# Expert weight loads of one expert with 8 KiB runs, in place of loads of two experts with 4 KiB runs

## The chip, the core and the metric

The program runs on one core of a Trainium2 chip. A core has the matrix engine (TensorE, PE in the profile, with its weight loads as PEld), the vector engine (DVE), the scalar engine (ACT), GpSimd (POOL) and the sync engine (SP), which here issues the DMAs; 16 DMA engines move the data. The metric is the device time of one execution in microseconds, 1385.64 us as the median of three.

## What is computed

Two layers of a decoder trunk on 512 tokens of 1024 channels. Each layer is a mixer (layer 0: gated mixing and a short convolution, layer 1: a gated linear recurrence) followed by a mixture of experts: 32 experts in 4 groups, each token goes to the two best experts of its best group. All weights are float32. The part that the change touches is the experts:

```python
def expert_block(args):                       # 128 slots of tokens, their gates, one expert
    tok_b, g_b, e = args
    xb = x_pad[tok_b]
    hid = jax.nn.silu(xb @ w_gate[e]) * (xb @ w_up[e])
    return (hid @ w_down[e]) * g_b[:, None].astype(xb.dtype)
# w_gate, w_up: (2, 32, 1024, 512); w_down: (2, 32, 512, 1024); the sum over a token's two slots is added to x
```

An expert's weights are three matrices of 2 MiB each. Both layers together read 2 x 32 x 6 MiB = 384 MiB of them; the mixers' weights are some 27 MiB.

## The kernel before

**Pairs.** Every expert has 64 slots for tokens, and two experts share one tile of 128 slots: `NPAIR` = 16 pairs a layer, numbered here from 0 to 15. `experts` (line 1057) works one pair: eight rows of `gate` into bank `pg`, eight of `up` into `pu`, the product `hid` (line 1072, one DVE instruction a pair), four transposes to `hT`, and four rows of `down` into `pd`, each row in two column halves. A row is what one partition holds of one contraction step: channel `8 p + j` for gate and up (`(p j)` with 8 rows of 512 numbers, 2 KiB each), `4 p + j` for down (4 rows of 1024 numbers, 4 KiB). `two` (line 1052) does both experts for one row: the expert `s` gets the partitions `64 s` to `64 s + 63` of the output, so every row needs the weights of both experts. Each call is one instruction in the program and two in the profile. Between `up` and `down` PE does work without weights: `gather` collects the tokens of the next pairs (`px`), `combine` adds the results of the pair before to the tokens (`pc`).

**Loads.** `moe_stream` (line 70) lists the loads of a layer in the order of use, `prefetch` (line 107) issues them on SP as buffers come free, `take` (line 126) hands the next one to the work and `done` (line 138) returns buffers and issues again. A load is 1 MiB: of both experts of a pair, two rows of gate or up, or one row of down. In DRAM these are two runs of 4 KiB a partition. A pair takes 12 loads: 4 gate, 4 up, 4 down. They lie in a ring of 12 buffers (10 of the tag `w`, and `D0`, `D1`; the first loads of a layer also use `Q` and `X`), and each buffer is returned when PE has done the load's rows. SP's queue is in order: it waits at the first load that has no buffer. In pair 0 gate and up are mixed by the table `FIRST`, since its tokens are gathered meanwhile. In the last pair `stop_at` keeps the next layer's loads back. `overflow` (line 1187) is a loop for experts with more than 64 tokens; it uses loads of its own, and the packets of the trace leave no room for a pass of it (126896 on the issue queue, all told for by the loads and stores outside of it).

The instructions stand in the order in which the program is written; there is no scheduler behind it.

Of the kernel before, what the change touches and what calls it, by code (L numbers as in the profile page):

```python
# [22 lines left out]
NJ = 8  # L23
NE = 32
CAP = 64
NPAIR = NE // 2
# [13 lines left out]
def hybrid_trunk(ctx: ExitStack, tc: tile.TileContext, x, norm_mix_g, norm_ffn_g, norm_final_g,  # L40
# [13 lines left out]
    def bank(i, name, shape=(P, 512), dtype=F32):  # L54
        return ps.tile(list(shape), dtype, tag=f"b{i}", name=name)
# [7 lines left out]
    def units(kind, u, src, slot="w"):  # L63
# [3 lines left out]
        for i in range(n):  # L67
            stream.append((kind, u, src[:, i * k:(i + 1) * k, :], slot))

    def moe_stream(l):  # L70
        slots = ["D1"] + ["w"] * RING + ["Q", "X"] + (["D0", "D1"] + ["w"] * RING) * (NPAIR + 1)
        n = 0
        for i in range(NPAIR):
            parts = [(w, NJ, t) for w in (moe_w_gate, moe_w_up) for t in range(4)]
            if i == 0:
                parts = [parts[k] for k in FIRST]
            for w, k, t in parts + [(moe_w_down, 4, t) for t in range(4)]:
                rows_of_both = w[l, 2 * i:2 * i + 2].rearrange("e (p j) f -> p e j f", j=k)
                stream.append(("moe", i, rows_of_both[:, :, t * k // 4:(t + 1) * k // 4, :], slots[n]))
                n += 1  # L80

    Y0 = (4, 5, 6, 7, 0, 1, 2, 3)
    Y1 = tuple(range(NJ))
# [54 lines left out]
    def done(n=1):  # L138

        for _ in range(n):  # L140
            free[used.popleft()] += 1
        prefetch()
# [614 lines left out]
    class Moe:  # L757
# [291 lines left out]
                G.tensor_tensor(self.rows[:, c, :].rearrange("t (p j) -> t j p", j=NJ), f(self.xh)[:, c],  # L1049
                                f(self.xl)[:, c], op=OP.add)  # L1050

        def two(self, o, xt, w, j, first, last, wide):
            for s in range(2):
                TE.matmul(o[64 * s:64 * s + 64, :], xt[:, 64 * s:64 * s + 64], w[s][:, j, wide],  # L1054
                          start=first, stop=last)

        def experts(self, xt, by, weights, done, between, during=lambda k, j: None, n=2, mixed=False, out="Q"):

            pg, pu = bank(0, "pg"), bank(1, "pu")
            for k, j in [divmod(n * part + i, NJ) for part in (FIRST if mixed else range(2 * NJ // n)) for i in range(n)]:  # L1060
                if j % n == 0:
                    w = weights(k, j // n)
                during(k, j)
                self.two((pg, pu)[k], xt()[:, j], w, j % n, j == 0, j == NJ - 1, slice(0, 512))
                if j % n == n - 1:
                    done()
                if (k, j) == (0, NJ - 1):
                    between(0)
                    sg = big.tile([P, 512], F32, tag="w1", name="sg")
                    A.activation(sg, pg, AF.Silu, scale=by(1))  # L1070
            hid = big.tile([P, 512], F32, tag="w2", name="hid")
            V.scalar_tensor_tensor(hid, pu, by(1), sg, op0=OP.mult, op1=OP.mult)  # L1072
            between(1)
            ptr = bank(4, "pth", (P, 4, P))
            for k in range(4):
                TE.transpose(ptr[:, k, :], hid.rearrange("s (f k) -> s k f", k=4)[:, k, :], ident)
            hT = big.tile([P, 4, P], F32, tag="w3", name="hT")
            A.copy(hT, ptr)  # L1078
            between(2)
            pd = [bank(2 + s, f"pd{s}") for s in range(2)]  # L1080
            for k in range(4):
                for s in range(2):
                    if n == 1:
                        w = weights(2, 2 * k + s)
                    elif s == 0:
                        w = weights(2, k)
                    self.two(pd[s], hT[:, k], w, 0, k == 0, k == 3,
                             slice(512 * s, 512 * s + 512) if n > 1 else slice(0, 512))
                done()
            between(3)  # L1090
            y = four(T, "y", F32R, out)
            yh, yl = y[0:2], y[2:4]
            for s in range(2):
                A.activation(yh[s], pd[s], AF.Copy, scale=by(0))  # L1094
                V.scalar_tensor_tensor(yl[s], pd[s], by(0), f(yh[s]), op0=OP.mult, op1=OP.subtract)  # L1095
            return yh, yl

        def blocks(self, after):

            steps = []  # L1100
            n_over = None
            for p in range(NPAIR):
                q, r = divmod(p, 2)
                sp = []
                if p == NPAIR - 1:

                    stop_at[0] = min(stop_at[0], pos[1] + 12 + AHEAD)

                rows = [lambda j=j: self.gather(q + 1, j)
                        for j in (range(4 * r, 4 * r + 4) if p > 1 else range(NJ) if p else ())] if q < NQ - 1 else []

                def whole(n):

                    for _ in range(n):
                        if rows:
                            rows.pop(0)()
                        if steps:
                            steps.pop(0)()  # L1120

                def during(k, j):
                    if (p, k, j) == (0, 1, 3):
                        self.gate_values()
                    if p == 0 and k == 0 and j % 2 == 0:
                        for i in (j, j + 1):
                            self.gather(0, i)

                def between(n):
                    if n == 0:  # L1130
                        if p == 0:
                            self.by_slot()
                        if r == 0 and q < NQ - 1:
                            self.spread(q + 1)
                        return
                    if n == 3 and self.l == 0 and p in (3, 4, 5):
                        lambda_constants(p - 3)
                    if n == 1:
                        for _ in range(min(2, len(rows))):
                            rows.pop(0)()  # L1140
                        if steps:
                            steps.pop(0)()
                    if n == 2:
                        while rows or steps:
                            whole(1)
                    if n == 3 and p == NPAIR - 1:
                        self.before_overflow()
                    if n == 3:
                        sp.append(self.place(pidx[:, p:p + 1], "w0" if p < NPAIR - 1 else "D0"))
                    if p == 0 and n == 1:  # L1150
                        self.slot_rows()
                        self.extras()

                if p == 3:
                    n_over = nc.values_load(self.cnt_i[0:1, 0:1], min_val=0, max_val=NOV // 2,
                                            skip_runtime_bounds_check_because="it is a sum of eight comparisons")
                def weights(k, part):
                    both = take("moe", p)
                    return [both[:, s] for s in range(2)]

                y = self.experts(lambda: self.xt[q][:, :, r * P:(r + 1) * P], lambda g: self.gs[:, g, p:p + 1],
                                 weights, done, between, during, mixed=p == 0)
                steps = self.combine(sp[0], *y, after if p == NPAIR - 1 else None)
                if p == NPAIR - 2 and self.l:
                    self.gain = gain_row(112, 6, "J")
            self.overflow(n_over)
            stop_at[0] = len(stream)
            free["D0"] = free["D1"] = free["Q"] = free["X"] = 0
            free["C1"] = 1
            prefetch()  # L1170
            warm(AF.Sqrt)
            for t in steps:
                t()
# [13 lines left out]
        def overflow(self, n_over):  # L1187

            slot, by, col, nxt, eid = self.walk
            with tc.For_i(0, n_over, 1):  # L1190
# [10 lines left out]
                for j in range(NJ):  # L1201
                    self.gather(NQ, j, P, lambda c: so[c // 2][:, c % 2])

                def loaded(k, part):
                    src, n = ((moe_w_gate, NJ), (moe_w_up, NJ), (moe_w_down, 4))[k]
                    j, h = (part, 0) if k < 2 else divmod(part, 2)
                    w = []
                    for s in range(2):
                        w.append(big.tile([P, 1, 512], F32, tag=f"sm{s + 1}", name="wo"))
                        e = src[self.l][bass.ds(ids[s], 1)].rearrange("o (p j) f -> p (o j) f", j=n)  # L1210
                        SY.dma_start(w[s], e[:, j:j + 1, 512 * h:512 * h + 512])
                    return w

                for t in self.combine(self.place(col), *self.experts(lambda: self.xt[NQ], lambda g: by[:, g, 0:1], loaded,
                                                         lambda: None, lambda n: None, n=1, out="C0")):
                    t()
                V.tensor_scalar(slot, slot, float(P), None, op0=OP.subtract)
                V.tensor_scalar(col, col, float(P), None, op0=OP.add)
# [175 lines left out]
```

## Time and profile before

| what | us |
|---|---|
| median of three runs | 1385.64 (1383.78 to 1388.72) |
| the profiled execution | 1385.47 |
| its span, first to last instruction | 1383.8 |
| PE busy | 1319.3 |
| DVE, ACT busy | 586.9, 347.2 |

The span is that of the profiled execution; 1.7 us lie around it. The expert stages take about 200 to 690 us (layer 0) and 890 to 1380 us (layer 1), the mixers the rest. In a window's row the letter x stands before the number of instructions, and matmuls are pipelined with their ends modelled, so a busy PE need not be a PE at its peak. A DMA share of 1.03 comes from packets that overlap on their engine.

### The profile page before, as it was taken

How to read it: one execution, taken by the hardware profiler on the slowest of the kernel's cores; microseconds unless marked ns; L12 is line 12 of the kernel's file. 1: busy time of each engine (PE TensorE's matmuls, PEld its weight loads, DVE VectorE, ACT ScalarE, POOL GpSimd, SP SyncE). 2: the span in 40 equal slices, each digit the busy share in tenths (PEclk: the TensorE clock that was granted, in tenths of full speed). 3: DMA queues.
4: the chain of work that ended last, by engine and by line, in shares of the span. 5: the costliest groups of instructions: out<-in, count | busy, mean ns of one | idle time of the engine just before them, and what ended most of it. 6: DMA issues, size and time to landing. Idle time of an engine off the chain costs nothing. (4 is left out here: it accounts for less than half of the span.)

```text
span 1383.8 us, 16540 instructions
## 1 busy us (share of the span) xinstructions
PE 1319.3 (95%) x6654; PEld 756.5 (55%) x6654; DVE 586.9 (42%) x1126; ACT 347.2 (25%) x581; POOL 49.4 (4%) x43
## 2 busy tenths in 40 slices
PE   9999999999999999998799999899999999999995
PEld 7888874554444544443486678545444454444432
DVE  6455462334323242322477873723333233323225
ACT  4335331121111211110246663212111111111113
POOL 0000200000000000000101001300000000000001
PEclk9999999999999999999899999999999999999998
DMA  9621169899999999999770035598999999999994
GB/s 358 202 97 61 61 230 339 346 410 408 410 409 409 409 409 409 409 409 409 274 267 0 0 143 202 207 347 335 409 410 408 409 409 409 409 409 409 409 409 161
DMA packets 126980, 436.95 MB, mean 316 GB/s; under 512 B 11316, under 2 KB 14000, under 8 KB 126896
## 3 DMA queue, kind: packets, MB, share of 16 engines
q1 hardware_dynamic: 126896, 435.82, 81.0%
q8 instruction: 55, 0.90, 0.3%
q14 instruction: 29, 0.24, 0.0%
HBM read 433.69 MB, written 2.10 MB: 315 GB/s over the span
## 5 line engine op out<-in xcount | busy, mean ns | idle before, releaser
L1054 PE MATMUL pu<-w,xt 128*64 128x512 f32 x1024 | 234.0, 597 | 20.7 <-DMA w<-in_moe_w_up_dram 19.3
L1054 PE MATMUL pg<-w,xt 128*64 128x512 f32 x1024 | 228.8, 597 | 3.7 <-ACT xt L916 2.5
L1054 PE MATMUL pd<-w,hT 128*64 128x512 f32 x1024 | 226.8, 595 | 1.4 <-ACT hT L1078 1.4
L1072 DVE SCALAR_TENSOR_TENSOR hid<-pu,gs,sg 128x512 f32<-128x512 f32 x32 | 24.0, 751 | 365.3 <-PE pu L1054 246.2
L1054 PEld LDWEIGHTS pu<-w,xt 128*64 128x64 f32 x1024 | 69.8, 137 | 178.1 <-issue 118.5
L1054 PEld LDWEIGHTS pg<-w,xt 128*64 128x64 f32 x1024 | 72.6, 137 | 147.5 <-issue 133.9
L1054 PEld LDWEIGHTS pd<-w,hT 128*64 128x64 f32 x1024 | 70.7, 137 | 140.4 <-issue 129.4
L916 ACT ACTIVATE xt<-px,gcol 128x256 f32<-128x256 f32 x128 | 60.7, 475 | 301.5 <-PE px L914 301.5
L913 PE MATMUL px<-st,xh 128*128 128x256 f32 x512 | 132.4, 294 | 1.9 <-DVE st L903 1.5
L914 PE MATMUL px<-st,xl 128*128 128x256 f32 x512 | 126.3, 282 | 0.0
L913 PEld LDWEIGHTS px<-st,xh 128*128 128x128 f32 x512 | 97.4, 190 | 30.9 <-issue 27.0
L1094 ACT ACTIVATE y<-pd,gs 128x512 fp32r<-128x512 f32 x64 | 43.8, 687 | 264.6 <-PE pd L1054 263.2
L1095 DVE SCALAR_TENSOR_TENSOR y<-pd,gs,y 128x512 fp32r<-128x512 f32 x64 | 47.8, 750 | 140.5 <-ACT y L1094 138.0
L1039 DVE TENSOR_TENSOR xT<-pc,xT 128x512 f32<-128x512 f32 x128 | 81.4, 684 | 57.1 <-PE pc L1038 57.1
L1039 DVE TENSOR_TENSOR rows<-pc,rows 128x512 f32<-128x512 f32 x128 | 81.1, 684 | 53.2 <-PE pc L1038 53.2
L914 PEld LDWEIGHTS px<-st,xl 128*128 128x128 f32 x512 | 97.5, 190 | 1.6
L405 DVE TENSOR_TENSOR wl<-w,wh 128x512 fp32r<-128x512 f32 x89 | 60.9, 687 | 51.9 <-PE pu L450 26.8
L1038 PE MATMUL pc<-sp,y 128*128 128x512 f32 x256 | 69.8, 406 | 4.7 <-issue 4.7
L404 ACT CAST wh<-w 128x512 fp32r<-128x512 f32 x94 | 58.0, 620 | 63.9 <-PE pu L450 37.7
L1070 ACT ACTIVATE sg<-pg,gs 128x512 f32<-128x512 f32 x32 | 22.0, 688 | 193.3 <-PE pg L1054 186.2
L1038 PE MATMUL pc<-y,sp 128*128 128x512 f32 x256 | 67.4, 395 | 2.0 <-DVEq L1190 2.0
L737 PE MATMUL po<-y,wh 128*128 128x512 f32 (+1 forms) x288 | 67.6, 376 | 0.7 <-ACT y L479 0.7
(264 smaller groups left out, 1357.4 us busy)
## 6 DMA issues: line engine op xcount, KB each, us to landing
w<-in_moe_w_gate_dram SPq DMA_DIRECT2D x128, 1024.0 KB, 18.3
w<-in_moe_w_up_dram SPq DMA_DIRECT2D x128, 1024.0 KB, 18.4
w<-in_moe_w_down_dram SPq DMA_DIRECT2D x128, 1024.0 KB, 18.3
w<-in_ab_w_in_dram SPq DMA_DIRECT2D x10, 1024.0 KB, 15.7
w<-in_c_w_in_dram SPq DMA_DIRECT2D x8, 1024.0 KB, 10.8
w<-in_ab_w_out_dram SPq DMA_DIRECT2D x4, 1024.0 KB, 10.0
w<-in_c_w_out_dram SPq DMA_DIRECT2D x4, 1024.0 KB
xin<-in_x_dram SPq DMA_DIRECT2D x4, 512.0 KB, 6.4
```

Of the source, the lines that this page charges most:

```text
L404: A.copy(wh, w)
L405: lo.tensor_tensor(wl, w, f(wh), op=OP.subtract)
L737: TE.matmul(o[m, i], w[:, kk, :], part(js[4 * kh + kk])[:, h], start=kh + k + kk == 0, stop=(kh, k, kk) == (1, 2, 3))
L913: TE.matmul(px, self.xh[:, c, j, :], st(c), start=(c == 0), stop=False)
L914: TE.matmul(px, self.xl[:, c, j, :], st(c), start=False, stop=(c == NT - 1))
L916: A.activation(self.xt[q][:, j, :], px, AF.Copy, scale=g)
L1038: TE.matmul(pc, a, b, start=(n == 0), stop=(n == 1))
L1039: V.tensor_tensor(d, pc, d, op=OP.add)
L1054: TE.matmul(o[64 * s:64 * s + 64, :], xt[:, 64 * s:64 * s + 64], w[s][:, j, wide], start=first, stop=last)
L1072: V.scalar_tensor_tensor(hid, pu, by(1), sg, op0=OP.mult, op1=OP.mult)
L1094: A.activation(yh[s], pd[s], AF.Copy, scale=by(0))
L1095: V.scalar_tensor_tensor(yl[s], pd[s], by(0), f(yh[s]), op0=OP.mult, op1=OP.subtract)
```

## The change

A load becomes one expert's: four rows of gate or up, or two rows of down, so 8 KiB a partition in one run. The size stays 1 MiB, the number of loads stays 12 a pair, and two consecutive loads (expert 0, expert 1) hold what two loads held before. `single` names the exceptions, which keep the old form: all of pair 0 and the four down loads of pair 15. `weights` now keeps the couple that is in use in `held`, and `read` returns both buffers when the last row of the couple is done.

```diff
+    def single(i, k):
+        return i > 0 and (i < NPAIR - 1 or k < 2)
     def moe_stream(l):
...
+            for k, w, t in [parts[k] for k in FIRST] + parts[8:] if i == 0 else parts:
+                n = (2, 2, 1)[k]
+                both = w[l, 2 * i:2 * i + 2].rearrange("e (p j) f -> p e j f", j=4 * n)
+                if single(i, k):
+                    pieces.append((i, both[:, t % 2, t // 2 * 2 * n:(t // 2 + 1) * 2 * n, :]))
+                else:
+                    pieces.append((i, both[:, :, t * n:(t + 1) * n, :]))
...
-                def weights(k, part):
-                    both = take("moe", p)
-                    return [both[:, s] for s in range(2)]
+                held = {}
+                def weights(k, j):
+                    r, h = divmod(j, 2) if k == 2 else (j, 0)
+                    n = (2, 2, 1)[k] * (2 if single(p, k) else 1)
+                    if r % n == 0 and not h:
+                        held[k] = [take("moe", p) for _ in range(2 if single(p, k) else 1)]
+                    t = slice(512 * h, 512 * h + 512)
+                    return [held[k][s][:, r % n, t] if single(p, k) else held[k][0][:, s, r % n, t] for s in range(2)]
+                def read(k, r):
+                    if (r + 1) % ((2, 2, 1)[k] * (2 if single(p, k) else 1)) == 0:
+                        done(len(held[k]))
```

The rest of the diff passes a row's weights to `two` already cut, and calls `done(k, j)` after every row instead of after every load.

On SP the list of loads keeps its length and order; only their form changes. These are the loads of pair 0 (from the second half of its up) and pair 1 before; 128x2x1024 is 128 partitions, two runs, 1024 numbers.

```order
L120 DMA w<-in_moe_w_up_dram 128x2x1024 x2
L120 DMA w<-in_moe_w_down_dram 128x2x1024 x4
L120 DMA w<-in_moe_w_gate_dram 128x2x1024 x4
L120 DMA w<-in_moe_w_up_dram 128x2x1024 x4
L120 DMA w<-in_moe_w_down_dram 128x2x1024 x4
```

The same place after:

```order
L127 DMA w<-in_moe_w_up_dram 128x2x1024 x2
L127 DMA w<-in_moe_w_down_dram 128x2x1024 x4
L127 DMA w<-in_moe_w_gate_dram 128x2048 x4
L127 DMA w<-in_moe_w_up_dram 128x2048 x4
L127 DMA w<-in_moe_w_down_dram 128x2048 x4
```

From pair 1 on a load is one run of 2048 numbers; pair 0 is as it was.

On PE the matmuls, their number and their order stay; the waits for loads move. This is the gate of pair 4 and the first row of its up before, with what each instruction waits for (DMAHW0 to DMAHW7 are the semaphores of the loads, in turn):

```order
L1054 MATMUL pg<-w,xt 64x512 [waits DMAHW6_49,Activation_49]
L1054 MATMUL pg<-w,xt 64x512 x3
L1054 MATMUL pg<-w,xt 64x512 [waits DMAHW7_49]
L1054 MATMUL pg<-w,xt 64x512 x3
L1054 MATMUL pg<-w,xt 64x512 [waits DMAHW0_49]
L1054 MATMUL pg<-w,xt 64x512 x3
L1054 MATMUL pg<-w,xt 64x512 [waits DMAHW1_49]
L1054 MATMUL pg<-w,xt 64x512 x3
L1054 MATMUL pu<-w,xt 64x512 [waits DMAHW2_49,PE_49]
```

And after:

```order
L1061 MATMUL pg<-w,xt 64x512 [waits DMAHW6_49,Activation_49]
L1061 MATMUL pg<-w,xt 64x512 [waits DMAHW7_49]
L1061 MATMUL pg<-w,xt 64x512 x6
L1061 MATMUL pg<-w,xt 64x512 [waits DMAHW0_49]
L1061 MATMUL pg<-w,xt 64x512 [waits DMAHW1_49]
L1061 MATMUL pg<-w,xt 64x512 x6
L1061 MATMUL pu<-w,xt 64x512 [waits DMAHW2_49,PE_49]
```

Before, each load is waited for by the first of its four matmuls. After, the first two matmuls of eight wait for one load each, and six follow without a wait.

## Rows read from the trace of the kernel before

**Rows 1.** the page: busy shares, 40 slices of DMA share and rate, one kind of load

```profile
PE 1319.3 (95%) x6654; PEld 756.5 (55%) x6654; DVE 586.9 (42%) x1126; ACT 347.2 (25%) x581; POOL 49.4 (4%) x43
...
DMA  9621169899999999999770035598999999999994
...
GB/s 358 202 97 61 61 230 339 346 410 408 410 409 409 409 409 409 409 409 409 274 267 0 0 143 202 207 347 335 409 410 408 409 409 409 409 409 409 409 409 161
...
w<-in_moe_w_gate_dram SPq DMA_DIRECT2D x128, 1024.0 KB, 18.3
```

**Rows 2.** windows: length, busy us by engine, granted clock, DMA share, GB/s

```profile
15.00:30.00 15.00, 15.00 (x68) 12.42 (x67) 11.62 (x18) 6.50 (x12) 0.00 (x0) 1.00 1.05 387
...
270.00:450.00 180.00, 180.00 (x927) 87.09 (x922) 63.23 (x125) 30.57 (x53) 0.00 (x0) 1.00 1.03 409
...
450.00:640.00 190.00, 181.82 (x908) 85.16 (x908) 61.87 (x105) 27.60 (x49) 0.00 (x0) 1.00 1.03 409
...
980.00:1140.00 160.00, 160.00 (x824) 77.34 (x821) 52.67 (x94) 24.79 (x44) 0.00 (x0) 1.00 1.03 409
...
1140.00:1340.00 200.00, 191.49 (x952) 87.99 (x953) 63.54 (x107) 29.09 (x51) 0.00 (x0) 1.00 1.03 409
```

**Rows 3.** the instructions on `hid`, pairs 2 to 7 and 10 to 15, layer 0

```profile
L1072 DVE SCALAR_TENSOR_TENSOR hid<-pu,gs,sg x6: 750/751/751, 275.3 to 419.8; 128x512 f32<-128x512 f32 x6
...
L1072 DVE SCALAR_TENSOR_TENSOR hid<-pu,gs,sg x6: 749/751/752, 509.6 to 664.1; 128x512 f32<-128x512 f32 x6
```

**Rows 4.** PE's timeline, end of layer 0, last row layer 1: start, us, work, wait

```profile
654.45 1.94 PE L1054 MATMUL pu<-w,xt 128*64 128x512 f32 x8 [0.72 <-DMA w<-in_moe_w_up_dram]
...
659.47 1.94 PE L1054 MATMUL pu<-w,xt 128*64 128x512 f32 x8 [0.61 <-SPq L1190]
...
662.04 1.94 PE L1054 MATMUL pu<-w,xt 128*64 128x512 f32 x8 [0.63 <-SPq L1190]
...
668.79 7.09 PE L1054 MATMUL pd<-w,hT 128*64 128x512 f32 x32
...
1350.37 1.94 PE L1054 MATMUL pu<-w,xt 128*64 128x512 f32 x8 [0.62 <-DMA w<-in_moe_w_up_dram]
```

**Rows 5.** DMA packets by size in 15:30 (first row) and 270:450 (second)

```profile
DMA packets 2919, 5.80 MB, mean 387 GB/s; under 512 B 94, under 2 KB 94, under 8 KB 2918
...
DMA packets 19078, 73.65 MB, mean 409 GB/s; under 512 B 1121, under 2 KB 1121, under 8 KB 19069
```

**Rows 6.** windows of 4 us around the gap of pair 1, columns as in rows 2

```profile
252.00:256.00 4.00, 4.00 (x23) 2.43 (x23) 2.67 (x5) 0.95 (x2) 0.00 (x0) 1.00 0.30 119
...
256.00:260.00 4.00, 4.00 (x22) 1.32 (x20) 0.46 (x1) 0.00 (x0) 0.00 (x0) 1.00 0.64 203
...
260.00:264.00 4.00, 4.00 (x22) 1.41 (x20) 2.48 (x7) 1.38 (x2) 0.00 (x0) 1.00 0.91 338
```

**Rows 7.** SP's timeline of issues, pairs 2 and 3: start, us until last issue, load

```profile
256.32 5.52 SPq L120 DMA_DIRECT2D w<-in_moe_w_down_dram  x4
...
270.05 5.52 SPq L120 DMA_DIRECT2D w<-in_moe_w_up_dram  x4
...
285.22 3.80 SPq L120 DMA_DIRECT2D w<-in_moe_w_down_dram  x3
```

**Rows 8.** SP's waits in 240:258: us in total, times, longest us

```profile
SPq L120 <- PE pd L1054: 13.4, 1, 13.4
```

**Rows 9.** PE's timeline, one pair in full flow, columns as in rows 4

```profile
341.03 7.09 PE L1054 MATMUL pd<-w,hT 128*64 128x512 f32 x32
...
347.95 7.04 PE L1054 MATMUL pg<-w,xt 128*64 128x512 f32 x32
...
354.82 7.04 PE L1054 MATMUL pu<-w,xt 128*64 128x512 f32 x32
```

More of the change, by code (lines that the diff above doesn't have):

```diff
@@ L68, in units @@
             stream.append((kind, u, src[:, i * k:(i + 1) * k, :], slot))
+    def single(i, k):
+        return i > 0 and (i < NPAIR - 1 or k < 2)
     def moe_stream(l):
         slots = ["D1"] + ["w"] * RING + ["Q", "X"] + (["D0", "D1"] + ["w"] * RING) * (NPAIR + 1)
-        n = 0
+        parts = [(k, w, t) for k, w in enumerate((moe_w_gate, moe_w_up, moe_w_down)) for t in range(4)]
+        pieces = []
         for i in range(NPAIR):
[L74 to L80, printed above, removed]
+            for k, w, t in [parts[k] for k in FIRST] + parts[8:] if i == 0 else parts:
[5 more added lines that the diff above has]
+                    pieces.append((i, both[:, :, t * n:(t + 1) * n, :]))
+        for n, (i, src) in enumerate(pieces):
+            stream.append(("moe", i, src, slots[n]))
     Y0 = (4, 5, 6, 7, 0, 1, 2, 3)
@@ L1050, in token_rows, with two @@
                                 f(self.xl)[:, c], op=OP.add)
-        def two(self, o, xt, w, j, first, last, wide):
+        def two(self, o, xt, w, first, last):
             for s in range(2):
-                TE.matmul(o[64 * s:64 * s + 64, :], xt[:, 64 * s:64 * s + 64], w[s][:, j, wide],
-                          start=first, stop=last)
+                TE.matmul(o[64 * s:64 * s + 64, :], xt[:, 64 * s:64 * s + 64], w[s], start=first, stop=last)
         def experts(self, xt, by, weights, done, between, during=lambda k, j: None, n=2, mixed=False, out="Q"):
@@ L1060, in experts @@
             for k, j in [divmod(n * part + i, NJ) for part in (FIRST if mixed else range(2 * NJ // n)) for i in range(n)]:
-                if j % n == 0:
-                    w = weights(k, j // n)
                 during(k, j)
-                self.two((pg, pu)[k], xt()[:, j], w, j % n, j == 0, j == NJ - 1, slice(0, 512))
-                if j % n == n - 1:
-                    done()
+                self.two((pg, pu)[k], xt()[:, j], weights(k, j), j == 0, j == NJ - 1)
+                done(k, j)
                 if (k, j) == (0, NJ - 1):
@@ L1082, in experts @@
                 for s in range(2):
[L1083 to L1089, printed above, removed]
+                    self.two(pd[s], hT[:, k], weights(2, 2 * k + s), k == 0, k == 3)
+                done(2, k)
             between(3)
@@ L1156, in blocks @@
                                             skip_runtime_bounds_check_because="it is a sum of eight comparisons")
-                def weights(k, part):
-                    both = take("moe", p)
-                    return [both[:, s] for s in range(2)]
+                held = {}
[9 more added lines that the diff above has]
+                        done(len(held[k]))
                 y = self.experts(lambda: self.xt[q][:, :, r * P:(r + 1) * P], lambda g: self.gs[:, g, p:p + 1],
-                                 weights, done, between, during, mixed=p == 0)
+                                 weights, read, between, during, mixed=p == 0)
                 steps = self.combine(sp[0], *y, after if p == NPAIR - 1 else None)
@@ L1202, in overflow, with loaded @@
                     self.gather(NQ, j, P, lambda c: so[c // 2][:, c % 2])
-                def loaded(k, part):
+                def loaded(k, j):
                     src, n = ((moe_w_gate, NJ), (moe_w_up, NJ), (moe_w_down, 4))[k]
-                    j, h = (part, 0) if k < 2 else divmod(part, 2)
+                    j, h = (j, 0) if k < 2 else divmod(j, 2)
                     w = []
@@ L1211, in loaded @@
                         SY.dma_start(w[s], e[:, j:j + 1, 512 * h:512 * h + 512])
-                    return w
+                    return [t[:, 0] for t in w]
                 for t in self.combine(self.place(col), *self.experts(lambda: self.xt[NQ], lambda g: by[:, g, 0:1], loaded,
-                                                         lambda: None, lambda n: None, n=1, out="C0")):
+                                                         lambda k, j: None, lambda n: None, n=1, out="C0")):
                     t()
```

## The prediction

> **What bounds the kernel now.** I read four views, in this order.
>
> The page first: PE is busy 95% of the span, but the line of DMA shares stands at 9 through both long expert stretches and the rate there holds still at 408 to 410 GB/s [rows 1]. A rate that flat beside a varying PE load is the mark of a transfer path at its ceiling, so I did not stop at "PE 95%".
>
> Then the windows, stretch by stretch [rows 2]. In 270:450 PE is busy 180.00 of 180.00 us, in 450:640 only 181.82 of 190.00; layer 1 repeats it. DMA is at share 1.03 and 409 GB/s in every one. So each layer's expert stage has two halves: first PE never waits and eats up the loads' lead, then PE waits for loads.
>
> Third, the pace of pairs from `hid`, one instruction a pair. Six of them from 275.3 to 419.8 us make (419.8 - 275.3)/5 = 28.90 us a pair where PE sets the pace; six from 509.6 to 664.1 make 30.90 us [rows 3]. One pair is twelve loads of 1 MiB [rows 1], 12.58 MB; at 409 GB/s that is 30.77 us. DMA needs 1.9 us more a pair than PE does, and the stage ends when DMA is through.
>
> Fourth, PE's timeline at the end of layer 0: `pu` comes in groups of 8 matmuls, one load each, 2.57 us apart (659.47, 662.04), each after a wait of 0.6 to 0.7 us [rows 4]. The row at 654.45 and that of layer 1 put the wait to an `up` load; those at 659.47 and 662.04 name a line of SP that moves no data, and the unchanged spacing says load there too. The last of these groups releases everything that follows, in both layers. Hence the bound: the landing of each layer's last `up` load.
>
> **What is changed in a load, and its price.** Each load stays 1 MiB on 128 partitions. What changes is its runs: two of 4 KiB a partition before, one of 8 KiB after. The price of a run can be had from this trace, since it has two run lengths under a full queue.
> - 15:30 loads `ab_w_in`, 512 columns of a wider row, 2 KiB runs: 2918 - 94 = 2824 data packets in 15 us on 16 engines [rows 5], so one engine takes a packet every 15000 x 16/2824 = 84.99 ns.
> - 270:450 loads experts in 4 KiB runs: 19069 - 1121 = 17948 packets in 180 us [rows 5], 160.46 ns each.
>
> The second 2 KiB cost 160.46 - 84.99 = 75.47 ns (16 engines at that pace: 434 GB/s), and 84.99 - 75.47 = 9.52 ns are left as the price of a packet, whatever its length. An 8 KiB packet should then take 9.52 + 4 x 75.47 = 311.4 ns instead of 320.9 for two. A load has 16 packets of 4 KiB on each engine, so 8 fewer: 8 x 9.52 = 76 ns less a load, 2567 to 2491 ns, 409 to 421 GB/s. No row shows an 8 KiB run. The lower bound of the gain is 0 (the run is still handled in 4 KiB pieces, or something other than the packet sets 409); the upper is what PE allows, below. I take 76 ns, the line through the two lengths that are there.
>
> **How many loads it counts for.** Up to pair 1, DMA is held back by full buffers: it idles in 252:256 at share 0.30 and is back at 0.91 by 260:264 [rows 6]. The cause is in SP's queue: it issues a load at 256.32 [rows 7], when `pd` of pair 1 gives back its first slot, after waiting 13.4 us for it [rows 8]. Loads numbered from 0, twelve a pair, this is number 32 (the first `down` of pair 2, as the name in the row says); it fills the queue again, and from 33 to number 187 (the last `up` of pair 15) DMA is never let go. These are 155 loads: 155 x 76 ns = 11.8 us a layer. Pair 0 and the last four `down` loads keep 4 KiB runs; the fourth of the latter lands 4 x 2.57 = 10.3 us after the last `up`, and PE wants it 6.75 + 3/4 x 7.09 = 12.1 us after (it starts on them at 668.79 [rows 4]), so they stay hidden.
>
> **What the change takes back.** PE's instructions are the same in number, kind and order, and so are those of DVE, ACT and POOL; PE's waits move. A row needs both experts, so PE starts when the second load of a couple has landed, works four rows and returns two slots at once. PE spends 7.04 to 7.09 us on four loads in full flow [rows 9], 1.77 us a load. Two places pay for it:
> - The restart of DMA in pair 1: the first slot comes back after two loads' work instead of one, 1.77 us later. Behind that issue on SP stand only further loads. Bounds: 0.4 us (two loads go out at once, where before the restart ran at 0.64 and 0.91 of a full share [rows 6]) to 1.77; I take 1.77, the nearer row being the work on one load.
> - The end: after the last `up` has landed PE has four rows to do, not two: 1.77 us more, then `hid`, the transposes and the rest as before. Nothing hides it.
>
> Elsewhere it costs nothing as long as the queue stays full. The tightest place is the gap of pair 2: SP issues twelve loads from 256.32 to about 275.6 us and then nothing until 285.22 [rows 7]. In 256:260 DMA is busy 0.64 of 4 us [rows 6], so it starts some 1.4 us after the first issue, at 257.7, and has work until 257.7 + 12 x 2.57 = 288.5; the next load is there at 285.2 + 1.4 = 286.6, 1.9 us early. After: 257.7 + 1.77 + 12 x 2.49 = 289.4 against 286.6 + 1.77 = 288.4, 1.0 us early. Each later pair adds 12 x 2.49 - 28.9 = 1.0 us to that. Without this cover the first pairs would lose what they lack of it.
>
> What is late next: PE. If PE never waited, `hid` of pair 15 would come 13 pairs after pair 2, at 275.3 + 13 x 28.90 = 651.0, 13.1 us before today's 664.1. That caps the gain at 13.1 us a layer; DMA's own result, below, leaves `hid` at 655.8, so DMA still sets the end, and PE still waits 4.8 us, at 1.0 us a pair in about the last five.
>
> **The sum.** A layer: -11.8 + 1.77 + 1.77 = -8.3 us; `hid` of pair 15 goes from 664.1 to 655.8. What follows (combine, mixer, the stores at the end) is started by it and moves along. Two layers: -16.5 us. Of the profiled execution's 1385.47 us (span 1383.8) this leaves 1369.0, and of the median of 1385.64, which lies 0.2 above, 1369.1. I forecast **1369**, -1.2%.
>
> **The rivals.**
> 1. *409 GB/s is not a matter of packets* (slower). If an 8 KiB run is moved as two of 4 KiB, or another ceiling stands at 409, no load gets faster and only the coarser hand-over remains: 2 x (1.77 + 1.77) = +7.1 us, 1392.7. It decides wherever the saving is under 3.54 us/155 = 23 ns a load, that is under 413 GB/s. Against it: two run lengths give 387 and 409 [rows 2], and a fixed ceiling would give one number. For it: nothing here is longer than 4 KiB, and the change not doing what it says belongs to this case. The Trainium skill ("DMA: Bandwidth & Descriptors", Where 436 GB/s comes from) has the HBM side bind such loads at about 358 GB/s, by which run length could not matter here; the trace stands at 409, over that figure, so I give the rule itself little.
> 2. *Only a third of the 9.5 ns belongs to the packet*, the rest to how the 2 KiB rows lie (a wider matrix, rows far apart), which the expert loads do not share. Then 8 x 3.2 = 25 ns a load, 155 x 25 = 3.9 us against 3.5: 0.4 us a layer, 1384.9, not to be told from no change. For it: the two lengths come from different tensors. Against it no row stands but rows 2, where one price fits both stretches without a second cause. The Trainium skill (same page, Why small descriptors are slow) puts the price at some 3 cycles a packet and finds the merging of descriptors worth it only up to 256 bytes; an estimate from it with that page's 850 MHz is 3.5 ns, 28 ns a load and 1384.0. Rows 2 speak against it: by 3.5 ns the 2 KiB stretch would run some 2% below the 4 KiB one, and 387 lies over 5% below 409.
> 3. *PE's cap*: loads get so much faster, or restart and tail so much cheaper, that PE never waits: -13.1 us a layer, 1359.4. It needs over 107 ns a load with both costs as above, more than the line gives; for it stands only that the costs are taken at their upper ends.
>
> **How the numbers follow.** Forecast 0.70, with 1364 to 1374 as its own range (the restart at 0.4 us gives 1366.4, a tenth of the saving either way 2.4 us, and the runs before spread from 1383.78 to 1388.72). Rival 1: 0.12. Rival 2: 0.10. Rival 3: 0.08. A measurement here tells about 0.3%, 4.2 us, from no change. Faster: forecast and rival 3, 0.78; within 0.3%: rival 2, 0.10; slower: rival 1, 0.12. The range 1360 to 1386 leaves out rival 1 and a part of rival 3.
>
> **What would show it.** Half the q1 packets in the expert stretches and mean packets near 8 KiB: the change does what it says. About 421 GB/s in 270:450 with the share still at 1.03: the price of a packet is right; 409 means rival 1, 412 rival 2. The first `down` load of pair 2 issued near 258.1 us: the restart. A `pu` group of 16 matmuls, 3.5 us, before the last `hid`, and that `hid` near 655.8: the tail. PE full until after 500 us, not 450: the lead lasts longer. The forecast is wrong if the rate misses 421 by more than some 3 GB/s, or if DMA's share dips in the gaps of pairs 2 to 4.

## The result and the profile after

The changed kernel takes **1368.47 us** (median, 1366.57 to 1370.52), the kernel before 1385.56 beside it: a ratio of 0.9874 (95% interval 0.985 to 0.9899). A second measurement with its own runs of before gave 1367.99 against 1386.03, again 0.9874 (0.9859 to 0.9889). The forecast was 1369.

The profiled execution of the changed kernel took 1369.55 us, span 1367.9. From its page, to be laid beside [rows 1]: PE's busy time, the rate in 40 slices, the packets.

```profile
PE 1320.5 (97%) x6654; PEld 764.9 (56%) x6654; DVE 586.8 (43%) x1126; ACT 347.0 (25%) x581; POOL 49.5 (4%) x43
...
GB/s 356 194 114 62 62 198 334 329 422 421 421 422 420 421 421 420 421 420 421 255 277 0 0 127 203 225 312 344 420 421 420 421 421 420 421 421 421 421 419 125
...
DMA packets 81924, 436.95 MB, mean 319 GB/s; under 512 B 11316, under 2 KB 14000, under 8 KB 36784
```

PE works as long as before (1319.3 then), so the time did not come from PE. The flat stretches of the rate stand at 419 to 422 instead of 408 to 410, and most of the packets are now 8 KiB or more: 81924 - 36784 = 45140.

The windows, answering to [rows 2] (length, busy us by engine, granted clock, DMA share, GB/s), and the packets of 270:450, answering to [rows 5]:

```profile
270.00:450.00 180.00, 180.00 (x923) 86.51 (x920) 62.92 (x125) 30.28 (x52) 0.00 (x0) 1.00 1.01 421
450.00:640.00 190.00, 189.56 (x945) 90.81 (x946) 64.27 (x109) 29.25 (x51) 0.00 (x0) 1.00 1.01 421
970.00:1130.00 160.00, 160.00 (x820) 76.25 (x817) 53.48 (x95) 24.65 (x44) 0.00 (x0) 1.00 1.01 421
1130.00:1320.00 190.00, 189.75 (x952) 91.62 (x952) 64.25 (x108) 29.95 (x52) 0.00 (x0) 1.00 1.01 421
...
DMA packets 10404, 75.82 MB, mean 421 GB/s; under 512 B 1156, under 2 KB 1156, under 8 KB 1156
```

In 450:640 the profile shows PE idle for 8.2 us before and for 0.4 us now; the pace of `hid`, below, shows that loads still held PE up there by more than that. The packets give the price that the forecast rested on: 10404 - 1156 = 9248 of them in 180 us on 16 engines are 180000 x 16/9248 = 311.4 ns each. The forecast had 311.4.

The product `hid`, answering to [rows 3]: pairs 2 to 7, pairs 10 to 15, then all sixteen of layer 0 and of layer 1. The four numbers of interest are the start of the first and of the last instruction of each row.

```profile
L1076 DVE SCALAR_TENSOR_TENSOR hid<-pu,gs,sg x6: 750/750/752, 276.2 to 420.7; 128x512 f32<-128x512 f32 x6
L1076 DVE SCALAR_TENSOR_TENSOR hid<-pu,gs,sg x6: 750/751/752, 507.4 to 656.8; 128x512 f32<-128x512 f32 x6
L1076 DVE SCALAR_TENSOR_TENSOR hid<-pu,gs,sg x16: 750/751/752, 220.3 to 656.8; 128x512 f32<-128x512 f32 x16
L1076 DVE SCALAR_TENSOR_TENSOR hid<-pu,gs,sg x16: 750/751/752, 899.1 to 1335.9; 128x512 f32<-128x512 f32 x16
```

The kernel before, layers 0 and 1, in the same view:

```profile
L1072 DVE SCALAR_TENSOR_TENSOR hid<-pu,gs,sg x16: 749/751/755, 219.4 to 664.1; 128x512 f32<-128x512 f32 x16
L1072 DVE SCALAR_TENSOR_TENSOR hid<-pu,gs,sg x16: 749/751/752, 907.3 to 1352.4; 128x512 f32<-128x512 f32 x16
```

Where PE sets the pace a pair still takes (420.7 - 276.2)/5 = 28.9 us. Where loads set it, the pace went from 30.90 to (656.8 - 507.4)/5 = 29.88. From pair 0 to pair 15 it is 436.5 and 436.8 us; before it was 444.7 and 445.1. This span, from `hid` of pair 0 to `hid` of pair 15, is the ruler for all that follows: it holds the whole stretch in which the loads count, and nothing of the mixers. I call it the **expert span**.

PE's timeline at the end of layer 0 and of layer 1, answering to [rows 4]:

```profile
648.04 3.65 PE L1061 MATMUL pu<-w,xt 128*64 128x512 f32 x16 [1.30 <-DMA w<-in_moe_w_up_dram]
...
653.02 3.65 PE L1061 MATMUL pu<-w,xt 128*64 128x512 f32 x14 [1.33 <-SPq L1201]
...
661.47 7.09 PE L1061 MATMUL pd<-w,hT 128*64 128x512 f32 x32
...
1332.11 3.65 PE L1061 MATMUL pu<-w,xt 128*64 128x512 f32 x14 [1.32 <-DMA w<-in_moe_w_up_dram]
```

The last groups before `hid` are now of four rows (16 matmuls; two records are missing in those that say x14) and take 3.65 us, where two rows took 1.94. Each still follows a wait for loads: the end is still set by the landing of the last `up`.

SP's issues and its wait, answering to [rows 7] and [rows 8], and the windows after the restart, answering to [rows 6]:

```profile
258.92 4.24 SPq L127 DMA_DIRECT2D w<-in_moe_w_down_dram  x4
...
287.82 4.24 SPq L127 DMA_DIRECT2D w<-in_moe_w_down_dram  x4
...
SPq L127 <- PE pd L1061: 14.7, 1, 14.7
...
256.00:260.00 4.00, 4.00 (x20) 1.29 (x18) 1.32 (x3) 0.00 (x0) 0.00 (x0) 1.00 0.12 23
260.00:264.00 4.00, 4.00 (x22) 1.41 (x20) 1.59 (x4) 1.38 (x2) 0.00 (x0) 1.00 0.90 324
264.00:268.00 4.00, 4.00 (x22) 1.31 (x20) 2.89 (x8) 0.00 (x0) 0.00 (x0) 1.00 0.98 373
...
284.00:288.00 4.00, 4.00 (x19) 1.35 (x20) 2.80 (x5) 0.00 (x0) 0.00 (x0) 1.00 1.01 420
```

The first load of pair 2's `down` goes out at 258.92, not 256.32; in this execution `hid` of pair 0 came 0.9 us later than before (220.3 against 219.4), so 1.7 us of the 2.6 are the coarser hand-over. DMA moves 23 GB/s in 256:260 where it moved 203; a part of that is the 0.9 us (in 252:256 it moves 209 where it moved 119). In the gap of pair 2 (284:288, before the issue at 287.82) the rate does not dip.

### The profile page after: what moved, and what is told of

Read it like the earlier page. It is cut to its first block, busy times and chain, and to the rows that moved or that the text cites. A ratio compares the mean times of both kernels' runs of the same rounds, so it can differ in the third digit from the quotient of the medians.

```text
span 1367.9 us, 16540 instructions
## 1 busy us (share of the span) xinstructions
PE 1320.5 (97%) x6654; PEld 764.9 (56%) x6654; DVE 586.8 (43%) x1126; ACT 347.0 (25%) x581; POOL 49.5 (4%) x43
## 2 busy tenths in 40 slices
DMA packets 81924, 436.95 MB, mean 319 GB/s; under 512 B 11316, under 2 KB 14000, under 8 KB 36784
## 5 line engine op out<-in xcount | busy, mean ns | idle before, releaser
L1061 PEld LDWEIGHTS pu<-w,xt 128*64 128x64 f32 x1024 | 76.1, 137 | 156.0 <-issue 141.8
```

## The experiments

The theory, A: a packet has a fixed price of 9.5 ns whatever its length; fewer packets make a load 76 ns shorter; 155 loads a layer sit on the path; a restart and a tail take some of it back. The rivals: the gain comes from the coarser hand-over or from where the rows lie, not from the runs; the loads are not what sets the end; the two costs were never there and the gain per load is smaller. The table gives the expert span of layers 0 and 1, the stretch between them (`hid` of pair 15 in layer 0 to `hid` of pair 0 in layer 1) and the time; all spans are worked out from rows like those on `hid` above.

| kernel | expert spans, us | between, us | time, us | ratio to before (95%) |
|---|---|---|---|---|
| before | 444.7, 445.1 | 243.2 | 1385.56 | |
| after | 436.5, 436.8 | 242.3 | 1368.47 | 0.9874 (0.985 to 0.9899) |
| after_again | 436.5, 436.2 | 241.8 | 1367.99 | 0.9874 (0.9859 to 0.9889) |
| after_third | 436.4, 435.7 | 241.7 | 1367.39, one run | |
| e1_split_runs | 448.2, 447.7 | 242.0 | 1393.5 | 1.0056 (1.0034 to 1.0077) |
| e3_last_up_old | 436.0, 434.9 | 243.9 | 1368.39 | 0.9871 (0.985 to 0.9892) |
| e3b_tail_again | 434.2, 434.4 | 246.1 | 1367.79, one run | |
| e4_first_down_old | 436.1, 435.3 | 242.0 | 1367.58 | 0.9869 (0.9845 to 0.9892) |
| e5_both_old | 434.4, 434.1 | 243.8 | 1365.37 | 0.9847 (0.9834 to 0.9861) |
| e5b_both_again | 434.3, 433.5 | 241.6 | 1363.03, one run | |
| e6_every_second | 438.9, 438.7 | 242.3 | 1372.97 | 0.9918 (0.9902 to 0.9933) |
| e7_less_pe_before | 444.7, 444.2 | 239.0 | 1381.04 | 0.9971 (0.9959 to 0.9983) |

**The changed hand-over without the long runs (e1_split_runs).** Each load is still one expert's, PE still waits for couples and returns two buffers at once, but a load takes rows 0, 1, 4, 5 or 2, 3, 6, 7, so its runs are 4 KiB again; PE works the rows in that order.

```diff
-                    pieces.append((i, both[:, t % 2, t // 2 * 2 * n:(t // 2 + 1) * 2 * n, :]))
+                    rows = both[:, t % 2].rearrange("p (h c r) f -> p h c r f", c=2, r=n)
+                    pieces.append((i, rows[:, :, t // 2]))
```

> The changed kernel with its hand-over kept (one expert a load, couples of two loads, two buffers back at once) but 4 KiB runs again: a gate or up load takes rows 0, 1, 4, 5 or 2, 3, 6, 7 of one expert, a down load rows 0, 2 or 1, 3, and PE takes the rows in that order. Nothing else differs. Theory A (a packet has a price, the gain is its number): 409 GB/s in 300:450, some 127 thousand packets, and what is left is the coarser hand-over, 2 x 3.5 = 7 us over the kernel before: 1392.7, some 24 us over the changed kernel. Theory B (the gain is that a load reads one expert's block and not two blocks 2 MiB apart): 421 GB/s and the changed kernel's time, 1368.5.

1393.5 us; in 270:450, and `hid` in both layers:

```profile
270.00:450.00 180.00, 179.28 (x910) 86.67 (x908) 62.49 (x124) 30.27 (x52) 0.00 (x0) 1.00 1.03 409
...
DMA packets 19075, 73.65 MB, mean 409 GB/s; under 512 B 1117, under 2 KB 1117, under 8 KB 19066
...
L1078 DVE SCALAR_TENSOR_TENSOR hid<-pu,gs,sg x16: 750/751/752, 220.2 to 668.4; 128x512 f32<-128x512 f32 x16
...
L1078 DVE SCALAR_TENSOR_TENSOR hid<-pu,gs,sg x16: 750/751/752, 910.4 to 1358.1; 128x512 f32<-128x512 f32 x16
```

Rate and packets are those of before, and the kernel is slower than before: the hand-over alone costs (3.5 + 2.6)/2 = 3.05 us a layer. Against the changed kernel (436.35 us, mean of the six spans) the runs alone are worth 447.95 - 436.35 = 11.6 us a layer, 75 ns for each of 155 loads. That is theory A in both of its parts.

**Run lengths alone (e2_runs_alone).** A kernel of loads only: 1 MiB each on 128 partitions from the expert weights through 12 buffers of one ring, in stretches of one run length, and at the end 2 MiB loads with 16 KiB runs through four buffers. No experts are computed; it copies x to the output.

> Loads alone, no arithmetic (the output is a copy of x, all of the trunk is left out): one after the other 32 loads of 1 MiB with 1 KiB runs, 32 with 2 KiB, 32 with 4 KiB of one expert, 32 with 4 KiB of two experts (the form before), 32 with 8 KiB (the form after), 16 of 2 MiB with 16 KiB runs, twelve buffers deep (four for the last). Theory A, 9.5 ns a packet and 75.5 ns for 2 KiB: 347, 386, 408, 408, 421 and 427 GB/s. Theory B, the block read through is what counts: the one-expert 4 KiB stage runs at 421, as the 8 KiB one, and only the two-expert stage at 409. Theory C (the 2 KiB loads of the kernel before were slow by their layout, the price of a packet being a third): 385, 400, 409, 409, 412, no step of 12 between 4 and 8 KiB.

The windows inside each stretch, in order 1 KiB, 2 KiB, 4 KiB of one expert, 4 KiB of two experts, 8 KiB, 16 KiB (length, PE busy, granted clock, DMA share, GB/s):

```profile
15.00:80.00 65.00, 0.00 (x0) 1.00 1.10 348
110.00:165.00 55.00, 0.00 (x0) 1.00 1.05 387
195.00:240.00 45.00, 0.00 (x0) 1.00 1.02 408
275.00:325.00 50.00, 0.00 (x0) 1.00 1.03 410
355.00:400.00 45.00, 0.00 (x0) 1.00 1.01 422
440.00:475.00 35.00, 0.00 (x0) 1.00 1.01 429
```

One packet takes its bytes x 16 divided by the rate: 47.1, 84.7, 160.2 (at 409), 310.6 and 611.1 ns. The steps from 1 to 2 KiB and from 2 to 4 are 37.6 and 75.5 ns, from 4 to 8 and 8 to 16 150.4 and 300.5: in all of them 37.6 to 37.8 ns a KiB, and what is left over is 9.5 to 9.8 ns in each row, from 1 KiB to 16. The rates are given to 1 GB/s, so the last row is known only to 0.7 ns either way. The loads of one expert with 4 KiB runs are not faster than those of two (408 against 410), so reading one expert's block gains nothing by itself. The Trainium skill ("DMA: Bandwidth & Descriptors", Why small descriptors are slow) gives, as one of two costs of a short descriptor, a fixed overhead of some 3 cycles a packet, by that page's 850 MHz an estimate of 3.5 ns; the price measured here is nearly three times that. Longer runs still pay here at 8 and 16 KiB.

**Half a dose, and none of the costs (e6_every_second).** Only even pairs from 2 to 14 get 8 KiB runs.

```diff
-        return i > 0 and (i < NPAIR - 1 or k < 2)
+        return i > 0 and i % 2 == 0
```

> Half a dose: only pairs 2, 4, 6 .. 14 get 8 KiB runs; pair 1 and pair 15 stay as before, so neither the restart nor the tail is paid for. Theory A: pair 2 has 11 such loads behind the restart and the six others 12 each, 83 loads x 76 ns = 6.3 us a layer, 12.6 in all, 1385.1 - 12.6 = 1372.5 (the gain per load is the same, and nothing is taken back). Rival B, the gain needs a stretch of long runs without a break (for example because a packet of 4 KiB behind one of 8 KiB on a queue is slowed, or because the sum of costs and gains was right by accident): 1378 or more. Rival C, the two costs were never paid in the changed kernel, and a load saves only 8.3 / 155 = 54 ns: 83 x 54 ns = 4.5 us a layer, 1376.1. Rate in 270:450: A about 415 GB/s, C about 417 needs the same packet price and is told apart by the time alone.

1372.97 us, 0.5 from the 1372.5 that was expected of theory A, and 415 GB/s:

```profile
270.00:450.00 180.00, 180.00 (x923) 86.83 (x920) 63.24 (x125) 30.28 (x52) 0.00 (x0) 1.00 1.02 415
...
L1076 DVE SCALAR_TENSOR_TENSOR hid<-pu,gs,sg x16: 750/751/752, 219.8 to 658.7; 128x512 f32<-128x512 f32 x16
```

The spans, 438.9 and 438.7, are 6.1 us shorter than before. The 83 loads of the expectation are miscounted: the restart is at load 32, the first `down` of pair 2, so only three of pair 2's loads lie behind it, not 11, and 75 count. With them theory A gives 75 x 76 ns = 5.7 us a layer, a span of 439.2 and a time of 1373.7; rival C (54 ns a load, no costs) gives 440.9, rival B more. (The 417 GB/s that the expectation has for C are the rate with every load 54 ns shorter; with half of them it is 413.) The spans lie 0.4 us from A and 2.1 from C: 6.1 us are 81 ns for each of 75 loads. The gain goes with the number of loads, and it needs no unbroken row of long runs.

**Less work for PE in the kernel before (e7_less_pe_before).** The gather of the tokens of pairs 4 to 15 leaves out the low half of each token's value; the loads are the same.

```diff
+                half = 2 <= q < NQ
-                TE.matmul(px, self.xl[:, c, j, :], st(c), start=False, stop=(c == NT - 1))
+                if not half:
+                    TE.matmul(px, self.xl[:, c, j, :], st(c), start=False, stop=(c == NT - 1))
```

> The kernel before with less work for PE and the same loads: the gather of the tokens of pairs 4 to 15 leaves out the four matmuls with the low half of the tokens in each channel block, 6 x 8 x 4 matmuls a layer, an estimate of 22 us of PE's time a layer from the rows of the trace. Theory A (the landing of the last up load sets the end of each expert stage): the time stays, 1385 us within 0.3%, and PE's waits grow by what was taken away. Rival B (PE sets the end for a good part): 20 to 45 us faster. In between, by how much the end follows PE.

```profile
270.00:450.00 180.00, 172.59 (x835) 75.58 (x832) 63.86 (x126) 30.72 (x55) 0.00 (x0) 1.00 1.03 409
450.00:640.00 190.00, 172.94 (x805) 72.06 (x805) 61.10 (x105) 26.23 (x47) 0.00 (x0) 1.00 1.03 409
...
L1074 DVE SCALAR_TENSOR_TENSOR hid<-pu,gs,sg x16: 750/751/755, 219.5 to 664.2; 128x512 f32<-128x512 f32 x16
```

In these two windows PE works 16.3 us less than in [rows 2], and `hid` of pair 15 comes at 664.2, before 664.1: not a tenth of a microsecond of it reached the end of layer 0, and 0.9 us in layer 1. That is the bound as the forecast had it. The time did fall, by 5.0 us or 0.36% in the medians (ratio 0.9971), at the edge of the 0.3% that A allowed, but not in the expert stages: in the profiled executions 4.2 us of it lie between the layers (239.0 against 243.2), behind the expert stage. What made that stretch shorter was not tried further; PE's idle time between `pd` and the last `pc` of the layer is 2.03 us there and 4.72 before, and the granted clock of the 40 us behind the last `hid` is 0.96 and 0.87.

**Taking back the two costs (e3_last_up_old, e4_first_down_old, e5_both_old).** The last `up` weight of pair 15 in the old form (e3), the `down` weight of pair 1 in the old form (e4), both (e5).

```diff
-        return i > 0 and (i < NPAIR - 1 or k < 2)
+        return i > 0 and (i < NPAIR - 1 or k < 1)                        # e3_last_up_old
+        return i > 0 and (i < NPAIR - 1 or k < 2) and (i, k) != (1, 2)   # e4_first_down_old
+        return i > 0 and (i < NPAIR - 1 or k < 1) and (i, k) != (1, 2)   # e5_both_old
```

> The changed kernel, but the four up loads of pair 15 in the old form (two rows of each of two experts), so that after the last one lands PE has two rows to do, not four. Theory A (the end is set by that landing): 1.77 us less a layer for the rows, 4 x 76 ns more for the packets, 2 x 1.5 = 2.9 us less than the changed kernel, 1365.5; the last hid 1.5 us earlier after the last restart. Rival (the end is set by the down loads behind it, or by PE): no change, 1368.5.

> The changed kernel, but the four down loads of pair 1 in the old form, so that PE gives back the first buffer after one load's work and DMA restarts 1.77 us earlier. Theory A (from that restart on DMA never stops, and it sets the end): the first down load of pair 2 is issued 2.0 us after the first down matmul of pair 1 instead of 3.7, everything behind moves by up to 1.77 us a layer, 2 x 1.77 = 3.5 us less than the changed kernel, 1365.0; if the restart then runs one load at a time with gaps, as in the kernel before, 1.5 to 3.5. Rival (the lead built up before covers it): no change, 1368.5.

> Both places that pay for the coarser hand-over go back to loads of four 4 KiB rows' halves as before (the first down weight of pair 1's ring turn and the last up weight); all other loads keep 8 KiB. Theory A as the prediction priced it: the restart gives back 1.77 us and the tail 1.77 us a layer, less 8 loads a layer that lose 76 ns: 2 x (1.77 + 1.77 - 0.6) = 5.9 us below the changed kernel, 1362.6. Theory B, from the two single runs: the tail's 1.4 us a layer is there in the trace but the time does not show it, the restart is worth under 1 us in all: 1367 to 1368. If A, hid(15) comes about 433.5 us after hid(0); if B, 435 or more. Between them, about 1365, nothing is settled but that the tail does count.

> The changed kernel once more, as the measure for the runs beside it on the same chip. Theory A (one packet's fixed price, 155 loads quicker by 76 ns): 1368.5 us as first measured, hid of pair 15 some 436.5 us after hid of pair 0 in both layers. No rival here; what it tells is how far two measurements of one kernel lie apart, against which the two runs on the restart and the tail are read.

e3 and e4 showed nothing in their times (-0.1 and -0.9 us against 1368.47, where theory A had 1365.5 and 1365.0), which looked like the end of both costs. The traces say otherwise. **The restart**, in windows of 50 us from `hid` of pair 0 on, so all at the same point of the layer: the kernel before, then after (layers 0 and 1), then e4 (both layers).

```profile
219.40:269.40 50.00, 49.28 (x262) 24.07 (x262) 17.47 (x36) 10.07 (x18) 0.00 (x0) 1.00 0.91 341
...
220.30:270.30 50.00, 49.28 (x262) 24.06 (x262) 17.47 (x36) 10.07 (x18) 0.00 (x0) 1.00 0.86 327
899.10:949.10 50.00, 49.28 (x262) 24.15 (x264) 17.50 (x36) 10.07 (x18) 0.00 (x0) 1.00 0.86 332
...
220.30:270.30 50.00, 49.28 (x262) 24.15 (x264) 17.52 (x36) 10.06 (x18) 0.00 (x0) 1.00 0.89 341
898.40:948.40 50.00, 49.28 (x262) 24.15 (x264) 17.52 (x36) 10.07 (x18) 0.00 (x0) 1.00 0.89 340
```

With the coarse hand-over it is 327 and 332 (325, 333, 327 and 330 in the other two profiles of this kernel, mean 329), with the old one in pair 1 341 and 340 (343, 342, 340 and 340 in e5 and its repeat, mean 341). The 12 GB/s between them over 50 us are 0.60 MB, at 421 GB/s 1.4 us.

Not all of that reaches the end. In e4 DMA starts again 1.6 us earlier (SP's issue at 257.31 instead of 258.92), but the next gap is where it was: pair 2's `down` still returns two buffers at once, and SP issues there at 287.91 (287.82 in the changed kernel). The prediction's cover for that gap, 1.0 us, is then 0.6 us short, and the rate of DMA dips a second time. Windows of 12 us, from 66 us behind `hid` of pair 0 on, in e4, layers 0 and 1:

```profile
286.30:298.30 12.00, 12.00 (x58) 4.02 (x56) 2.12 (x3) 1.42 (x3) 0.00 (x0) 1.00 0.99 378
964.40:976.40 12.00, 12.00 (x58) 4.02 (x56) 2.12 (x3) 1.42 (x3) 0.00 (x0) 1.00 1.00 410
```

In the three profiles of the changed kernel these windows have 418 to 424 GB/s, in e5 and its repeat 378, 398, 388 and 413. The mean of the six with the old form in pair 1 is 394, 27 GB/s below the changed kernel's 421: 0.33 MB, 0.8 us of the 1.4. What a finer hand-over in pair 2 as well would give was not tried.

**The tail**: two rows again, 1.94 us (e5b_both_again, end of layer 0):

```profile
650.20 1.94 PE L1061 MATMUL pu<-w,xt 128*64 128x512 f32 x8 [0.60 <-SPq L1201]
...
652.76 1.94 PE L1061 MATMUL pu<-w,xt 128*64 128x512 f32 x8 [0.62 <-SPq L1201]
```

3.65 - 1.94 = 1.7 us, less 0.3 for four loads that are slow again. In the spans, against 436.35: e3 and its repeat 434.9 (-1.5), e4 435.7 (-0.65, where 1.4 - 0.8 leaves 0.6), e5 and its repeat 434.1 (-2.3; 433.5 expected, or 433.2 without the 0.3 us charged for pair 1's `down`, which lies before the restart). One kernel's spans differ by up to 1.8 us between executions (e3 and its repeat, layer 0), so the 0.65 of e4 rests on the rates, not on its two spans alone. The restart and the tail together, 1.4 + 1.7 = 3.1 us, are what e1 showed as the cost of the hand-over (3.05). And e5 is faster in time, though not down to theory A's 1362.6: its five runs of 1362.75 to 1365.83 all lie below the changed kernel's runs, 1366.3 to 1370.52. Its median is 2.6 us below that of after_again, less than the 2 x 2.3 of the spans.

**Where the rest went (e3b_tail_again, e5b_both_again, after_third).** In e3 and e5 the stretch between the layers had come out 1.5 to 2 us longer than in the changed kernel. The same kernels once more:

> The kernel with the old last up weight once more, one look, for the stretch between the layers (hid of pair 15 in layer 0 to hid of pair 0 in layer 1). Theory S (the stretch goes with the form of the last weight: the clock falls at another place when the stage ends in the old way): 243.8 us again, and the time near 1368. Theory R (the place where the clock falls differs from execution to execution): the stretch lies anywhere in the 241.8 to 243.9 us seen in the other kernels, here about 242, and the time near 1366.

> The kernel with both old places once more, one look. Theory S: the stretch between the layers 243.8 us again, time near 1365.4. Theory R: near 242 as in four of the five other kernels, time near 1363.5. The stretches within the layers as before in both, 434.2 us.

> The changed kernel a third time, one look, beside the two others. Theory S: 241.8 to 242.4 us between the layers again. Theory R: another value in 241.8 to 243.9.

246.1, 241.6 and 241.7 us: the same two kernels with another value than the first time (243.9 and 243.8), so the form of the last weight does not fix it, and 246.1 lies outside of theory R's range too. That the form has a part in it is not excluded: the five executions whose last `up` loads hold four rows of one expert (the changed kernel, e1, e4) lie in 241.7 to 242.3, the seven with two rows of both (the kernel before, e3, e5, e6, e7 and the repeats) in 239.0 to 246.1. The 40 us behind the last `hid` of layer 0, PE's busy time and granted clock, for e3, e3b, e5 and e5b:

```profile
655.90:695.90 40.00, 32.81 (x150) 0.87 0.79 277
...
654.10:694.10 40.00, 33.10 (x141) 0.79 0.82 289
...
654.40:694.40 40.00, 33.32 (x153) 0.87 0.81 289
...
654.80:694.80 40.00, 32.35 (x159) 0.96 0.81 287
```

PE idles between `pd` and the last `pc`, and behind that TensorE is granted 1.2 instead of 2.4 GHz for a part of the stretch. In the changed kernel, with PE idle for 2 us and then at the lower level (columns as in the windows above):

```profile
668.80:670.80 2.00, 0.00 (x0) 0.00 (x0) 1.17 (x2) 0.85 (x2) 0.00 (x0) 1.00 0.03 8
...
672.80:674.80 2.00, 0.99 (x2) 0.83 (x3) 0.00 (x0) 0.00 (x0) 0.00 (x0) 0.50 1.05 406
```

The part differs between executions: at 0.79 the stretch takes 246.1, at 0.87 243.9 and 243.8, at 0.96 241.6. The Trainium skill ("TensorE: Matmul & The Clock Gate", What's actually happening) says of a kernel's start that the point of the change of clock differs from run to run of one kernel; the trace agrees that it differs, here in the middle of one (0.87 and 0.79 for the kernel of e3, 0.87 and 0.96 for that of e5). The clock is not all of it: the changed kernel has 0.91, 0.87 and 0.87 with 242.3, 241.8 and 241.7. It does not settle it over the whole stretch either, where the granted clock is 0.95 in e5 and in after_third, with 243.8 and 241.7 us. What else is in the stretch stays open.

## Why the prediction was right

**The bound.** Right: e7 took PE work away and `hid` of pair 15 did not move; e6 shortened half of the loads and it moved by the loads' share.

**The packet price** (9.52 ns, 311.4 ns for 8 KiB, 421 GB/s). Right, from two run lengths of a trace that had no third; e2 has the same line from 1 to 16 KiB. That 311.4 ns came out to the digit is luck: the 2 KiB stretch has 2824 packets, and 16 more or fewer, one on each engine, move its 84.99 ns by 0.5. The first rival, a ceiling at 409, is out by 421 in the kernel and by 429 in e2. Both, like the 409 before, lie above the 358 GB/s at which the Trainium skill ("DMA: Bandwidth & Descriptors", Where 436 GB/s comes from) has the HBM side bind, a figure that it gets as one of two cores' share; here one core runs. The second, a third of the price, is out: it wanted 412. Its reasoning, that the 2 KiB rows lie otherwise than the expert rows, is out by e2, where all run lengths come from expert weights.

**155 loads.** Right within what the spans tell: 11.6 us a layer against 11.8 (after against e1), 81 ns a load in e6 against 76.

**The restart**, 1.77 us: 1.4, so somewhat overpriced; the value taken was the upper bound, and one layer of the six even had 333 GB/s in the 50 us, under 1 us lost. The cover in the gap of pair 2 was as forecast: none was lost there in the changed kernel, and with the restart 1.6 us earlier (e4) the rate dipped there. One reading on the way to it is off without harm: 1.44 us of idle time in 256:260 count from 256.00 and not from the issue at 256.32, so DMA began at 257.4, not at 257.7; both ends of the comparison move by it. **The tail**, 1.77: 3.65 - 1.94 = 1.7. Together the span was forecast to shrink by 8.3 us and shrank by 8.55 in the mean of the three profiles.

**PE's cap.** Right by the pace: with `hid` of pair 2 at 276.2, PE alone would have reached pair 15 at 276.2 + 13 x 28.9 = 651.9; it came at 656.8, 4.9 us later. The forecast had 4.8. The profile shows 2.8 us of waits for loads in that time; the rest does not show as idle time, in a PE that counts as busy but falls behind (144 matmuls in 508:537, 150 in the 29 us before).

**The signs.** `hid` of pair 15 at 656.8, forecast 655.8, with 0.9 us of it from before pair 0. SP's issue 1.7 us late, the group of 16, no dip in pair 2: as forecast. One sign was wrong: DMA's share fell from 1.03 to 1.01 where I expected it to stay. E2 has the same: the share goes down with the length of the run (1.10, 1.05, 1.03, 1.01), by some 4 to 5 ns a packet (0.10 x 47.1, 0.05 x 84.7, 0.03 x 160.2), so the overlap seems to be one of each packet, and to halve with their number. The rate was the sign to go by.

**The sum.** -16.5 us forecast, -17.1 and -18.0 measured. The spans give 2 x 8.55 = 17.1; the rest of the difference is no larger than the scatter of the stretch between the layers.

**Faster still.** e5_both_old is the changed kernel with the finer hand-over at the two places that pay for it: 1365.37 us, -1.5% against before, -0.2% against the changed kernel. If PE never waited from pair 2 on, the span would be 380.6 - 13 x 28.9 = 4.9 us shorter than the changed kernel's 436.5 (380.6 from `hid` of pair 2 to that of pair 15), 431.6; e5's 434.1 is 2.5 us a layer away from it.

## What to carry to other kernels

Where DMA holds one flat rate, read two run lengths of the trace as a line: time of a packet = price + bytes / slope; it tells what a longer run is worth before one is built, also above 4 KiB. Count the gain only over loads between the last time that the queue ran dry and the landing that PE waits for last, and keep the hand-over fine at those two ends; an earlier restart pays only as far as the next gap still has loads to cover it. To judge a change of 1 or 2 us, compare a span of the trace that the change can move, not the time alone, and take it more than once: here the stretch behind the stage scattered by up to 4.5 us, and the span itself by up to 1.8.

## What was not expected of the hardware

- An earlier restart of the queue was in part lost again 30 us later: e4 expected DMA never to stop behind it, and it fell to 378 and 410 GB/s in the gap of pair 2.
- The stretch between the layers differs by up to 4.5 us between executions of nearly the same work (241.6 to 246.1), with a granted clock of 0.96 to 0.79 in its first 40 us. It hid a gain of 1.5 us a layer in e3's time.
- The restart of the emptied queue did not cost the same in both layers of the same execution: 327 and 332, 325 and 333 GB/s over the same 50 us, 0.6 and 1 us apart. Why was not tried.
